# A hybrid attention block on one core: priority for the splits of the values, two heads written in place, a last block scaled on two engines, and residual scalings queued later

## The chip, the core and the metric

The kernel runs on one core of a Trainium2 chip. A core has a matrix engine (TensorE, PE in the profile, with its weight loads shown apart as PEld), a vector engine (VectorE, DVE), a scalar engine (ScalarE, ACT), a general engine (GpSimd, POOL) and a sync engine (SyncE, SP), which here issues nearly all DMAs. Matrix products are written to PSUM; everything else works from SBUF or PSUM; DRAM is reached by DMA. Each engine works through its own queue in order, and waits at its head for what it needs from the others. The metric is the device time of one execution in microseconds.

## The reference

One layer of a residual block, all in float32, on 512 positions of 2048 features:

```
h    = rmsnorm(x, g_attn)
proj = h @ w_in                       # 2048 x 6152: q, k, v of two kinds of heads, and f
o_sb  = stick_breaking_attention(qa, ka, va)       # 8 heads of 128, strictly causal
o_fox = forgetting_attention(qf, kf, vf, log_f)    # 8 heads of 128, causal
mixed = concat(head_rmsnorm(o_sb), head_rmsnorm(o_fox))
x = x + mixed @ w_out                 # 2048 x 2048
u = relu(rmsnorm(x, g_mlp) @ w_up)    # 2048 x 8192
x = x + (u * u) @ w_down              # 8192 x 2048
y = rmsnorm(x, g_final)
```

In stick-breaking attention the weight of a key is its logistic score times the product of (1 - score) of the keys between it and the query; in logarithms that is a running sum from right to left. Forgetting attention is a softmax with a bias that is the cumulative logarithm of a forget gate.

## The kernel before

**Precision.** Every operand of a product is split into a high part (a cast on ACT, line 60, or a scaled copy, line 63) and a low part (the difference, on DVE, line 61 or 64). `mm3` (lines 93 to 95) then makes three matmuls of high and low parts. One 512-column matmul is the unit of PE's work nearly everywhere.

**Order.** The program is written out without loops on the chip. A planner takes the instructions with their dependences and a priority each, which is program order, with blocks under `tc.high_priority()` ahead of everything else; it plays a modelled timeline and gives each engine, as it comes free, the ready instruction of the highest priority. The order so found is fixed for each engine's queue and for SP's. `with tc.issue_after(ins)` puts what the block holds on the engine of `ins` behind `ins` in that queue, without waiting for its end.

**Heads (lines 449 to 469).** The loop over `n` takes two heads a turn. `project` makes q and k of each (`project_q`, one PSUM bank `accq` of the pool `acc` of four banks, 48 matmuls). In turns 2, 6 and 10 `accumulate_v` makes the values of four heads at once in all four banks of `acc` (`accv`); in turn 14 it makes those of the last two. `take_v` splits them: for each of four row blocks and each pair of heads a scaled copy `vh` on ACT (line 63) and a low part `vl` on DVE (line 64). Only when both pairs of a row block are split is its bank free for the next `accq`. `attend` runs under high priority: `scores` into the one PSUM tile `s`, the weights `w` on ACT, DVE and POOL, transposes `pt` into the same PSUM tile, the split `ph`, `pl`, the product `o` with the values, and a norm (lines 291 to 303). Its result `os` is stored to DRAM, `md[h]` (line 304). Between the products, `drip` lets a side computation on DVE go on (`up_sums`, lines 153 to 161: sums of blocks of `w_up`, through two SBUF tiles `x0` and `x1`).

**Output projection (lines 512 to 555).** `mixed`, two tiles with the tags `x0` and `x1`, is loaded back from `md`, 16 DMAs (line 514). For each of four column blocks `n`, and each two heads `k0`, w_out is loaded and split, the two heads are split (`uh`, `ul`), and 24 matmuls add to `acco`. Column block 0 fills PE beside the last heads. Then x is added (line 534, DVE, `x2`), 16 transposes go to four PSUM tiles `tr`, ACT scales each by `g_up` into `hr` (line 547), and `a_form` makes the seven left-hand operands F of a Winograd form of the up projection, each with a split. Product 1 takes rows 0 to 255 of `hr` from the even transposes only; product 5 and its followers take sums of others. Squares of `x2` on ACT (line 555) follow. Of the last block, operands 4 and 3 are made later (line 761).

**Up and down projection (lines 579 to 827).** 32 `Unit`s make the hidden layer by seven products each (lines 619 and 621, 512 and 256 columns); PSUM tile `psa` is copied by ACT (line 625) between products 1, 6 and 7. The down projection takes the groups of `GROUPS` (two of three units, then six of four) for two halves `db`, each in seven products `second`, into two PSUM buffers `accd`; the first group copies them out on ACT (line 718), later ones add them on DVE (line 720).

**Residual.** The sum x2, stored in `xd`, is brought back in eight pieces by `add_residual` (lines 722 to 731): a load into a buffer `wraw` (three of them), two scalings by `v2` on ACT (line 728), one or two additions on DVE (729, 731). It is called from group 2 on, after the third product of each half, one piece at a time.

Of the kernel before, what the change touches and what calls it, by code (L numbers as in the profile page):

```python
# [11 lines left out]
ALU = mybir.AluOpType  # L12
# [23 lines left out]
def block_kernel(ctx, tc, x, g_attn, w_in, b_f, g_out_sb, g_out_fox, w_out, g_mlp, w_up, w_down, g_final, y):  # L36
# [16 lines left out]
    acc_cm = tc.tile_pool(name="acc", bufs=4, space=PSUM)  # L53
    acc = acc_cm.__enter__()

    lows = [None]

    def split(hi, lo, src, scale=None):
        if scale is None:
            ins = act.copy(hi, src)  # L60
            lows[0] = dve.tensor_tensor(lo, src, hi.bitcast(F32), op=ALU.subtract)  # L61
        else:
            ins = act.mul(hi, src, scale)
            dve.scalar_tensor_tensor(lo, src, scale, hi.bitcast(F32), op0=ALU.mult, op1=ALU.subtract)  # L64
        return ins
# [109 lines left out]
    with (  # L175
# [77 lines left out]
                pool.affine_select(out=d, in_=d, compare_op=op, fill=fill, base=0,  # L253
                                   pattern=[[0, n], [-1, P]] if n > 1 else [[-1, P]], channel_multiplier=1)

        def weigh(h, v, hc, w, gv, left=2):

            pt = atp.tile([P, 1536], F32, tag="s", name="pt")

# [43 lines left out]
            dve.scalar_tensor_tensor(os_, os_, gv, va, op0=ALU.mult, op1=ALU.mult)  # L303
            sp.dma_start(md[h], os_)

        def attend_sb(h, v, hc, q, k):
            s = scores(q, k)
            w = wide("w")
            act.activation(w, s, AF.Abs)
            act.activation(w, w, AF.Exp, scale=-1.0)  # L310
            act.activation(w, w, AF.Ln, bias=1.0)
            dve.scalar_tensor_tensor(w, s, 0.0, w, op0=ALU.max, op1=ALU.add)
            causal(w, ALU.is_gt, 0.0)
            for r in rows(w):

                dve.tensor_tensor_scan(r[:, ::-1], r[:, ::-1], r[:, ::-1], 0.0, op0=ALU.add, op1=ALU.max)
            dve.tensor_tensor(w, s, w, op=ALU.subtract)
            act.activation(w, w, AF.Exp)
            causal(w, ALU.is_gt, 0.0)
            weigh(h, v, hc, w, g_sb[:, h:h + 1], NH - 1 - h)  # L320

        def attend_fox(h, v, hc, q, k):
# [19 lines left out]
            weigh(NH + h, v, hc, w, g_fx[:, h:h + 1])  # L342

        o0 = 3 * WSB
        order = [NH + h for h in (6, 7, 0, 1, 2, 3, 4, 5)] + list(range(NH))
# [69 lines left out]
        with tc.tile_pool(name="attp", bufs=1, space=PSUM) as atp:  # L415
# [33 lines left out]
            for n in range(0, 2 * NH, 2):  # L449
# [5 lines left out]
                def attend(i, qk):  # L455
                    h = order[n + i]
                    with tc.high_priority():
                        (attend_fox if h >= NH else attend_sb)(h % NH, v, i, *qk)

                qk = [project(0), project(1)]  # L460

                if n == 2 * NH - 2:
                    vs = take_v(accumulate_v([v_columns(order[n])], 2 * P, [4] * 4))
                elif n % 4 == 2:
                    c = [v_columns(order[n + i]) for i in (0, 2)]
                    vs = take_v(accumulate_v(c[:1] if c[1] == c[0] + 2 * P else c, 4 * P, [2] * 8), 2)
                v = vs.pop(0)
                for i in range(2):
                    attend(i, qk[i])
# [39 lines left out]

    A_ORDER = (1, 4, 5, 6, 2, 7, 3)  # L510

    mixed = [mixp.tile([P, NH, NT], F32, tag=f"x{i}", name="mixed") for i in range(2)]
    for k in range(2 * NH):
        sp.dma_start(mixed[k // NH][:, k % NH, :], md[order[k]])

    for n in range(4):
        ns = slice(n * NT, (n + 1) * NT)
        ps = [acc.tile([P, NT], F32, tag="acc", name="acco") for _ in range(TB)]
# [14 lines left out]
        for t in range(TB):  # L533
            dve.tensor_tensor(x2[:, t, :], x2[:, t, :], ps[t], op=ALU.add)
        hr = xp.tile([P, 2, 2, NT], F32, tag="hr", name="hr")
        for i in range(4):
            tr = trp.tile([P, NT], F32, tag="tr", name="tr1")

            for t in ((TB - 1, *range(TB - 1)) if n < 3 else range(TB)):
# [4 lines left out]
                if i == 0 and t == TB - 1:  # L544
                    first_turn = turn_
            k = 4 * n + i
            act.mul(hr[:, i // 2, i % 2, :], tr, g_up[:, k:k + 1])
        sp.dma_start(xd[n], x2)
        s12 = xp.tile([P, 2, 2 * P], F32, tag="s12", name="s12")
        for p in (1, 5, 6, 2, 7, 4, 3):  # L550
            if n == 3 and p == 4:
                break
            a_form(p, hr, form_parts(p, n), s12)
        for t in range(TB):
            act.activation(x2[:, t, :], x2[:, t, :], AF.Square, accum_out=ss2[:, t, n:n + 1])
# [166 lines left out]
    def add_residual(p, db):  # L722
# [1 line left out]
        t0, j = {2: (0, 0), 3: (0, 1), 4: (1, 0), 7: (1, 1)}[p]  # L724
        r = wp.tile([P, 2, NT], F32, tag="wraw", name="xr")
        sp.dma_start(r, xd[2 * j + db][:, 2 * t0:2 * t0 + 2, :])
        for t in range(2):
            act.mul(r[:, t], r[:, t], v2[:, 2 * t0 + t:2 * t0 + t + 1])
        dve.tensor_tensor(M[p][:, :, db, :], M[p][:, :, db, :], r, op=ALU.add)
        if p == 7:  # L730
            dve.tensor_tensor(M[4][:, :, db, :], M[4][:, :, db, :], r, op=ALU.subtract)
# [198 lines left out]
```

## Time and profile before

| | us |
|---|---|
| median of three runs (2093.44, 2096.15, 2096.15) | 2096.15 |
| the profiled execution's own time | 2093.38 |
| its span | 2091.7 |

The span falls into stages, here with PE's idle time in each:

| stage | from, to (us) | PE idle | DVE busy | ACT busy |
|---|---|---|---|---|
| opening, first values | 0, 50 | 4.9 | 60% | 61% |
| heads | 50, 609 | 8.2 | 70% | 42% |
| output projection, last heads beside it | 609, 828 | 2.9 | 63% | 55% |
| up projection | 828, 1458 | 2.9 | 81% | 65% |
| down projection | 1458, 2037 | 5.9 | 86% | 43% |
| end | 2037, 2091.7 | 9.1 | 62% | 36% |

The mean granted clock of PE over the span is 0.996. To read the tables: a stage in which PE is idle for 1% of the time is set by PE's own work, and what can be changed there is only where and why it stands still. In rows of the timeline the columns are the start, the duration, engine and line, operation, what it writes and reads, and in brackets the idle time of the engine just before with what ended it. In tables by stretch the columns are the stretch, its length, busy time and number of instructions of PE, PEld, DVE, ACT and POOL, the granted clock, the DMA share and GB/s.

### The profile page before, as it was taken

How to read it: one execution, taken by the hardware profiler on the slowest of the kernel's cores; microseconds unless marked ns; L12 is line 12 of the kernel's file. 1: busy time of each engine (PE TensorE's matmuls, PEld its weight loads, DVE VectorE, ACT ScalarE, POOL GpSimd, SP SyncE). 2: the span in 40 equal slices, each digit the busy share in tenths (PEclk: the TensorE clock that was granted, in tenths of full speed). 3: DMA queues.
4: the chain of work that ended last, by engine and by line, in shares of the span. 5: the costliest groups of instructions: out<-in, count | busy, mean ns of one | idle time of the engine just before them, and what ended most of it. 6: DMA issues, size and time to landing. Idle time of an engine off the chain costs nothing.

```text
span 2091.7 us, 26837 instructions
## 1 busy us (share of the span) xinstructions
PE 2057.8 (98%) x10292; PEld 1748.8 (84%) x10292; DVE 1604.4 (77%) x1825; ACT 1068.5 (51%) x1428; POOL 65.5 (3%) x77
## 2 busy tenths in 40 slices
PE   9999999998999999999999999999999999999998
PEld 8888888887888787888888888888788888888886
DVE  6767767676866565788788787788698988888886
ACT  6334343354455555666666666666644443333433
POOL 0000000010110000000000000000000000000003
PEclk9999999999999999999999999999999999999999
DMA  8997986966843444577777787788856665664731
GB/s 252 338 321 220 327 269 215 338 190 228 292 153 100 161 135 154 195 260 258 247 265 258 242 267 249 249 266 301 281 202 248 247 223 176 245 246 140 266 116 81
DMA packets 361761, 482.10 MB, mean 230 GB/s; under 512 B 12017, under 2 KB 255777, under 8 KB 351521
## 3 DMA queue, kind: packets, MB, share of 16 engines
q1 hardware_dynamic: 360672, 478.26, 68.1%
q10 hardware_dynamic: 960, 2.13, 0.3%
q8 instruction: 81, 1.33, 0.3%
q14 instruction: 48, 0.39, 0.1%
HBM read 360.28 MB, written 120.06 MB: 230 GB/s over the span
## 4 chain that ended last, share of the span: by engine, by line
PE 90%; DVE 4%; DMA 3%; ACT 1%; issue 1%; SPq 0%; ACTq 0%; DVEq 0%
PE psa L619 11%; PE accd L94 7%; PE accd L95 7%; PE accd L93 7%; PE psa L621 6%; PE accq L93 5%; PE psc L619 5%; PE accq L95 5%; PE accq L94 5%; PE psc L621 3%; PE acco L93 3%; PE acco L95 3%; PE acco L94 3%; PE psb L619 3%; PE accv L93 3%; PE accv L95 2%
## 5 line engine op out<-in xcount | busy, mean ns | idle before, releaser
L61 DVE TENSOR_TENSOR wl<-wu,wh 128x1024 fp32r<-128x1024 f32 x166 | 201.7, 1219 | 35.0 <-ACT wh L60 21.3
L60 ACT CAST wh<-wd 128x1024 fp32r<-128x1024 f32 (+1 forms) x136 | 134.5, 999 | 165.3 <-PE accd L95 105.4
L60 ACT CAST wh<-wraw 128x1024 fp32r<-128x1024 f32 (+2 forms) x133 | 135.5, 1019 | 157.9 <-PE accq L94 86.5
L60 ACT CAST wh<-wu 128x1024 fp32r<-128x1024 f32 x166 | 173.7, 1049 | 79.4 <-PE psa L619 19.0
L93 PE MATMUL accq<-hH,wh 128*128 128x512 f32 x512 | 201.1, 393 | 7.7 <-DVE vl L64 7.7
L95 PE MATMUL accq<-hH,wl 128*128 128x512 f32 x512 | 201.2, 393 | 0.0
L94 PE MATMUL accq<-hL,wh 128*128 128x512 f32 x512 | 200.6, 392 | 0.0
L61 DVE TENSOR_TENSOR wl<-wraw,wh 128x1024 fp32r<-128x1024 f32 (+2 forms) x133 | 157.7, 1187 | 49.0 <-ACT wh L60 48.6
L61 DVE TENSOR_TENSOR wl<-wd,wh 128x1024 fp32r<-128x1024 f32 (+1 forms) x136 | 155.6, 1153 | 44.5 <-ACT wh L60 43.9
L93 PE MATMUL accd<-wh,uf 128*128 128x512 f32 x436 | 169.8, 390 | 1.0 <-issue 1.0
L94 PE MATMUL accd<-wl,uf 128*128 128x512 f32 x436 | 169.6, 389 | 0.0
L95 PE MATMUL accd<-wh,uf 128*128 128x512 f32 x436 | 169.6, 389 | 0.0
L60 ACT CAST wx<-wd 128x1024 fp32r<-128x1024 f32 (+1 forms) x88 | 87.6, 1000 | 125.2 <-PE accd L95 73.0
L93 PEld LDWEIGHTS accq<-hH,wh 128*128 128x128 f32 x512 | 96.7, 189 | 28.2 <-issue 8.5
L61 DVE TENSOR_TENSOR wx<-wd,wx 128x1024 fp32r<-128x1024 f32 (+1 forms) x88 | 100.7, 1153 | 21.3 <-ACT wx L60 21.0
L93 PE MATMUL accd<-wx,uf 128*128 128x512 f32 x284 | 110.6, 390 | 3.4 <-ACT m L718 3.4
L94 PEld LDWEIGHTS accq<-hL,wh 128*128 128x128 f32 x512 | 96.7, 189 | 19.9
L95 PEld LDWEIGHTS accq<-hH,wl 128*128 128x128 f32 x512 | 96.6, 189 | 19.9
L94 PE MATMUL accd<-wx,uf 128*128 128x512 f32 x284 | 110.6, 390 | 0.2 <-DVE wx L61 0.2
L720 DVE TENSOR_TENSOR m<-m,accd 128x1024 f32<-128x1024 f32 x84 | 102.1, 1216 | 11.0 <-PE accd L95 10.9
L95 PE MATMUL accd<-wx,uf 128*128 128x512 f32 x284 | 110.5, 389 | 0.0
L619 PE MATMUL psa<-fl,wh 128*128 128x512 f32 x388 | 107.0, 391 | 2.6 <-DVE fl L61 2.6
(312 smaller groups left out, 4865.5 us busy)
## 6 DMA issues: line engine op xcount, KB each, us to landing
ufd<-st SPq DMA_DIRECT2D x98, 512.0 KB, 5.2
sums<-in_w_up_dram SPq DMA_DIRECT2D x96, 512.0 KB, 6.0
td<-sums SPq DMA_DIRECT2D x32, 1536.0 KB, 8.2
wd<-in_w_down_dram SPq DMA_DIRECT2D x48, 1024.0 KB, 7.1
wu<-td SPq DMA_DIRECT2D x95, 512.0 KB, 4.9
wraw<-in_w_in_dram SPq DMA_DIRECT2D x84, 512.0 KB, 5.9
uf<-ufd SPq DMA_DIRECT2D x42, 1024.0 KB, 6.9
wu<-in_w_up_dram SPq DMA_DIRECT2D x32, 1024.0 KB, 7.8
```

The source lines that it names most:

```text
L60: ins = act.copy(hi, src)
L61: lows[0] = dve.tensor_tensor(lo, src, hi.bitcast(F32), op=ALU.subtract)
L93: pe.matmul(out, sh, mh, start=first, stop=False, skip_group_check=True)
L94: pe.matmul(out, sh, ml, start=False, stop=False, skip_group_check=True)
L95: pe.matmul(out, sl, mh, start=False, stop=last, skip_group_check=True)
L619: pe.matmul(ps, hi[:, a, :], both, start=a == 0 and p in (1, 2, 5), stop=False, skip_group_check=True)
L621: pe.matmul(ps[:, :2 * P], lo[:, a, :], F[p][a // 4][:, a % 4, 0, :], start=False, stop=a == KC // 2 - 1, skip_group_check=True)
L720: dve.tensor_tensor(M[p][:, :, db, :], M[p][:, :, db, :], ps, op=ALU.add)
```

## The change

There are four edits.

1. The splits of `take_v` in turns 2, 6, 10 and 14 are traced under `tc.high_priority()`, as the attention is. The products of the values before them are not.
2. `mixed` is allocated in turn 14, before the last two heads' attention, and 14 of the 16 loads stand there. The last two heads write the last step of their norm (line 303) straight into `mixed[1]`, without store and load.
3. In the last of the four column blocks the transposes are taken in the order 0, 2, 1, 3; tiles 1 and 3 are scaled on DVE (`tensor_scalar`) instead of ACT; and `a_form(1)` is traced right after tile 2, ahead of tiles 1 and 3. The remaining operands follow in the same order as before.
4. The two scalings of `add_residual` are put behind the last unscaled cast that `split` made (`casts[0]`), which at that point of the program is a cast of the same half's third product. The loads and additions are not bound.

```diff
-    lows = [None]
+    lows, casts = [None], [None]
@@ def split
-            ins = act.copy(hi, src)
+            ins = casts[0] = act.copy(hi, src)
@@ def weigh
-            dve.scalar_tensor_tensor(os_, os_, gv, va, op0=ALU.mult, op1=ALU.mult)
-            sp.dma_start(md[h], os_)
+            out = os_ if here is None else here
+            dve.scalar_tensor_tensor(out, os_, gv, va, op0=ALU.mult, op1=ALU.mult)
+            if here is None:
+                sp.dma_start(md[h], os_)
@@ def attend
-                        (attend_fox if h >= NH else attend_sb)(h % NH, v, i, *qk)
+                        (attend_fox if h >= NH else attend_sb)(h % NH, v, i, *qk, mixed[1][:, NH - 2 + i, :] if n == 2 * NH - 2 else None)
...
                 if n == 2 * NH - 2:
-                    vs = take_v(accumulate_v([v_columns(order[n])], 2 * P, [4] * 4))
+                    ps = accumulate_v([v_columns(order[n])], 2 * P, [4] * 4)
+                    with tc.high_priority():
+                        vs = take_v(ps)
+                    mixed = [mixp.tile([P, NH, NT], F32, tag=f"x{i}", name="mixed") for i in range(2)]
+                    for k in range(2 * NH - 2):
+                        sp.dma_start(mixed[k // NH][:, k % NH, :], md[order[k]])
                 elif n % 4 == 2:
                     c = [v_columns(order[n + i]) for i in (0, 2)]
-                    vs = take_v(accumulate_v(c[:1] if c[1] == c[0] + 2 * P else c, 4 * P, [2] * 8), 2)
+                    ps = accumulate_v(c[:1] if c[1] == c[0] + 2 * P else c, 4 * P, [2] * 8)
+                    with tc.high_priority():
+                        vs = take_v(ps, 2)
...
-    mixed = [mixp.tile([P, NH, NT], F32, tag=f"x{i}", name="mixed") for i in range(2)]
-    for k in range(2 * NH):
-        sp.dma_start(mixed[k // NH][:, k % NH, :], md[order[k]])
@@ for n in range(4)
-        for i in range(4):
+        last = n == 3
+        for i in (0, 2, 1, 3) if last else range(4):
             tr = trp.tile([P, NT], F32, tag="tr", name="tr1")
...
             k = 4 * n + i
-            act.mul(hr[:, i // 2, i % 2, :], tr, g_up[:, k:k + 1])
+            if last and i % 2:
+                dve.tensor_scalar(hr[:, i // 2, i % 2, :], tr, g_up[:, k:k + 1], None, op0=ALU.mult)
+            else:
+                act.mul(hr[:, i // 2, i % 2, :], tr, g_up[:, k:k + 1])
+            if last and i == 2:
+                a_form(1, hr, form_parts(1, n))
         sp.dma_start(xd[n], x2)
         s12 = xp.tile([P, 2, 2 * P], F32, tag="s12", name="s12")
-        for p in (1, 5, 6, 2, 7, 4, 3):
-            if n == 3 and p == 4:
-                break
+        for p in (5, 6, 2, 7) if last else (1, 5, 6, 2, 7, 4, 3):
             a_form(p, hr, form_parts(p, n), s12)
@@ def add_residual
-        for t in range(2):
-            act.mul(r[:, t], r[:, t], v2[:, 2 * t0 + t:2 * t0 + t + 1])
+        with tc.issue_after(casts[0].ins):
+            for t in range(2):
+                act.mul(r[:, t], r[:, t], v2[:, 2 * t0 + t:2 * t0 + t + 1])
```

More of the change, by code (lines that the diff above doesn't have):

```diff
@@ L254, in causal, with weigh @@
                                    pattern=[[0, n], [-1, P]] if n > 1 else [[-1, P]], channel_multiplier=1)
-        def weigh(h, v, hc, w, gv, left=2):
+        def weigh(h, v, hc, w, gv, here, left=2):
             pt = atp.tile([P, 1536], F32, tag="s", name="pt")
@@ L302, in weigh, with attend_sb @@
             dve.scalar_tensor_tensor(va, va, 1.5, ra, op0=ALU.subtract, op1=ALU.mult)
-            dve.scalar_tensor_tensor(os_, os_, gv, va, op0=ALU.mult, op1=ALU.mult)
-            sp.dma_start(md[h], os_)
-        def attend_sb(h, v, hc, q, k):
+            out = os_ if here is None else here
+            dve.scalar_tensor_tensor(out, os_, gv, va, op0=ALU.mult, op1=ALU.mult)
+            if here is None:
+                sp.dma_start(md[h], os_)
+        def attend_sb(h, v, hc, q, k, here):
             s = scores(q, k)
@@ L319, in attend_sb, with attend_fox @@
             causal(w, ALU.is_gt, 0.0)
-            weigh(h, v, hc, w, g_sb[:, h:h + 1], NH - 1 - h)
-        def attend_fox(h, v, hc, q, k):
+            weigh(h, v, hc, w, g_sb[:, h:h + 1], here, NH - 1 - h)
+        def attend_fox(h, v, hc, q, k, here):
             ck = atp.tile([P, NT], F32, tag="o", name="ck")
@@ L341, in attend_fox @@
                 dve.tensor_scalar(r, r, l[:, i:i + 1], None, op0=ALU.mult)
-            weigh(NH + h, v, hc, w, g_fx[:, h:h + 1])
+            weigh(NH + h, v, hc, w, g_fx[:, h:h + 1], here)
         o0 = 3 * WSB
```

## The prediction, made before the changed kernel was run

> **What bounds the kernel now.** I read three views in this order: the engines' busy time, PE's waits by line, and short stretches behind each wait. The page's first part:
>
> ```profile
> PE 2057.8 (98%) x10292; PEld 1748.8 (84%) x10292; DVE 1604.4 (77%) x1825; ACT 1068.5 (51%) x1428; POOL 65.5 (3%) x77
> ```
>
> PE is the bound nearly everywhere: of 2091.7 us it stands still for 33.9. No edit takes work off PE, so all there is to win lies in those 33.9 us and in what follows them. PE's waits, longest first:
>
> ```profile
> PE accq L93 <- DVE vl L64: 7.7, 1, 7.7
> PE accd L93 <- ACT m L718: 3.4, 2, 2.1
> PE trg L353 <- DMA g_rows<-in_g_attn_dram: 3.3, 1, 3.3
> PE acco L93 <- ACT uh L60: 2.9, 1, 2.9
> PE psa L619 <- DVE fl L61: 2.6, 1, 2.6
> ```
>
> Four of these five are what the edits touch, one each: I call them S1 (7.7, low parts of values), S2 (2.9, heads read back), S3 (2.6, the last block's first operand) and S4 (2.1, a copy on ACT); the fifth is the opening. A wait costs more than itself. In stretches of 2 us (the figure before the DMA share is the granted clock) right behind S1, S2, S3 and S4, with a calm stretch last:
>
> ```profile
> 500.00:502.00 2.00, 2.00 (x5) 1.62 (x6) 2.00 (x4) 0.66 (x1) 1.11 (x2) 0.50 0.64 190
> 502.00:504.00 2.00, 2.00 (x6) 1.52 (x6) 1.94 (x4) 0.00 (x0) 0.00 (x0) 0.52 1.07 442
> 688.00:690.00 2.00, 2.00 (x7) 1.53 (x6) 0.15 (x1) 0.58 (x1) 0.00 (x0) 0.56 0.79 305
> 690.00:692.00 2.00, 2.00 (x7) 1.52 (x6) 2.00 (x4) 0.91 (x2) 0.00 (x0) 0.59 0.00 0
> 834.00:836.00 2.00, 1.51 (x7) 1.39 (x8) 2.00 (x4) 2.00 (x7) 0.00 (x0) 0.75 1.07 354
> 836.00:838.00 2.00, 2.00 (x9) 1.81 (x9) 2.00 (x5) 2.00 (x7) 0.00 (x0) 0.50 1.11 375
> 838.00:840.00 2.00, 2.00 (x13) 1.82 (x12) 1.74 (x5) 2.00 (x3) 0.00 (x0) 0.89 1.02 413
> 1484.00:1486.00 2.00, 1.15 (x5) 0.97 (x6) 0.22 (x1) 2.00 (x3) 0.00 (x0) 1.00 1.05 409
> 1700.00:1750.00 50.00, 50.00 (x222) 41.39 (x221) 46.96 (x36) 21.92 (x23) 0.00 (x0) 1.00 0.77 281
> ```
>
> PE counts as busy in them, but at half clock. The lost time is the missing clock times the length: S1 2 x (0.50 + 0.48) = 2.0; S2 2 x (0.44 + 0.41) = 1.7; S3 2 x (0.25 + 0.50 + 0.11) = 1.7; S4 nothing. So the four cost 9.7, 4.6, 4.3 and 2.1, together 20.7 us.
>
> The Trainium skill (TensorE: Matmul & The Clock Gate, section "Why this matters for your kernels") says that idle gaps over about 3 us bring the clock down to half. By that rule the gaps of S2 and S3 would have cost only themselves and the four together 17.3 us. The trace differs: the clock was 0.56 behind a wait of 2.9 us and 0.50 behind one of 2.6, and I go by the trace.
>
> **Edit 1, the splits of the values.** S1 in detail, DVE's queue first:
>
> ```profile
> 488.20 0.47 ACT L63 ACTIVATE vh<-accv,r1v 128x256 fp32r<-128x256 f32 x1
> ```
> ```profile
> 488.96 1.54 DVE L158 TENSOR_TENSOR sums<-sums 128x1024 f32<-128x1024 f32 x1
> 490.42 0.77 DVE L61 TENSOR_TENSOR pl<-ph,pl 128x512 fp32r<-128x512 f32 x1
> 491.12 2.64 DVE L316 TENSOR_TENSOR_SCAN w<-w 128x256 f32<-128x256 f32 x3
> 493.69 0.45 DVE L64 SCALAR_TENSOR_TENSOR vl<-accv,r1v,vh 128x256 fp32r<-128x256 f32 x1
> ```
> ```profile
> 499.22 0.86 DVE L64 SCALAR_TENSOR_TENSOR vl<-accv,r1v,vh 128x256 fp32r<-128x256 f32 x2
> ```
> ```profile
> 491.75 0.40 PE L297 MATMUL ssq<-pl,onesr 128*128 128x512 f32 x1
> 499.83 0.77 PE L93 MATMUL accq<-hH,wh 128*128 128x512 f32 x1 [7.68 <-DVE vl L64]
> ```
>
> The first high part of the values is there at 488.67; its low part waits 5 us behind a block sum, an attention split and scans, and the bank's last low part runs at 499.22, while PE wants the bank at about 492.1. With priority the first low part goes ahead of the block sum, at about 489.0; the second cast and low part (0.47 and 0.45 us) follow by about 490.9 even behind the `pl` of 0.77. The bank is free 1.2 us before PE asks. S1 goes: -9.7; if the planner leaves the order, 0. Nothing is added; block sums move back, and nobody waits for them here. The eight casts wait on ACT for PE's rows of values, as they do now; behind them stand casts of projection weights, one of which serves 24 matmuls, 24 x 50/222 = 5.4 us. The scans yield to at most eight low parts, 8 x 0.45 = 3.6 us: the head gets that much later in its place, and is priced as a rival.
>
> **Edit 2, two heads in place.**
>
> ```profile
> 678.60 0.74 DVE L303 SCALAR_TENSOR_TENSOR os_last<-os_last,g_rest,ph 128x512 f32<-128x512 f32 x1
> ```
> ```profile
> 679.37 0.34 SPq L304 DMA_DIRECT2D md<-os_last  x1
> 683.32 0.34 SPq L514 DMA_DIRECT2D mixed<-md  x1
> ```
> ```profile
> 686.13 0.62 ACT L60 CAST uh<-mixed 128x512 fp32r<-128x512 f32 x1 [1.80 <-DMA mixed<-md]
> ```
>
> The last head is finished at 679.34; store and load take until 686.13. In place, its cast can end at 679.34 + 0.7 = 680.0, while PE has other work until 686.80 - 2.90 = 683.9. The wait goes with 3.9 us to spare: -4.6; at worst 0, if the head itself comes late against PE (a rival). Four DMAs leave SP. The 14 other loads stand earlier in program order, past the last two heads' stores on SP's queue, but need the tiles that `sums` holds until its last use, so they cannot start sooner than now; each costs SP 0.34 us.
>
> **Edit 3, the last block.**
>
> ```profile
> 828.82 2.42 ACT L547 ACTIVATE hr<-tr,g_rest 128x512 f32<-128x512 f32 x4 [5.81 <-PE tr L543]
> ```
> ```profile
> 831.28 0.69 DVE L501 TENSOR_TENSOR s<-hr 128x512 f32<-128x512 f32 x1 [3.19 <-ACT hr L547]
> ```
> ```profile
> 834.49 0.80 PE L619 MATMUL psa<-fl,wh 128*128 128x512 f32 x2 [2.61 <-DVE fl L61]
> ```
> ```profile
> 837.12 0.58 ACT L625 COPY s<-psa 128x512 f32<-128x512 f32 x1
> ```
> ```profile
> 838.95 1.09 PE L619 MATMUL psa<-fh,wh 128*128 128x512 f32 x4
> ```
> ```profile
> 2086.47 0.48 DVE L870 TENSOR_SCALAR m<-m,v 128x512 f32<-128x512 f32 x1
> ```
>
> Four scalings of 0.61 run in a row, then sums, then splits, until PE gets the low part at 834.49; it wanted it at 831.9. Now ACT scales two tiles by 828.82 + 1.21 = 830.0, casts operand 1 (0.62) by 830.7, DVE subtracts (0.69) by 831.4: in time. DVE's two scalings from PSUM occur nowhere in the trace; the nearest rows are 0.48 (the same operation from SBUF) and 0.69 (an addition of that size). I take 0.69, the longer, as these read PSUM; both end at about 830.2 beside ACT's, so DVE's sums start 1.1 us sooner than at 831.28. What is late next: before product 6 PE needs ACT's copy of `psa`, now at 837.12 to 837.70 behind an unbroken row of ACT's work. PE comes 4.3 us sooner, at 838.95 - 4.3 = 834.7; the copy comes only by the two scalings sooner, at 837.7 - 1.2 = 836.5. A wait of 1.8 us stays, of S4's size, which left the clock alone. So -2.5, with 0 and -4.3 as ends.
>
> **Edit 4, the residual.**
>
> ```profile
> 1477.09 1.57 ACT L60 CAST wx<-wd 128x1024 fp32r<-128x1024 f32 x2
> 1482.57 1.33 ACT L728 ACTIVATE xr<-xr,v 128x512 f32<-128x512 f32 x2 [3.92 <-DMA xr<-xd]
> 1483.81 0.99 ACT L718 COPY m<-accd 128x1024 f32<-128x1024 f32 x1
> ```
> ```profile
> L729 DVE TENSOR_TENSOR m<-m,xr 128x1024 f32<-128x1024 f32 x8 | 9.8, 1220 | 0.0
> ```
>
> ACT takes up a scaling in group 0, waits 3.92 us for its load, and the copy that frees `accd` stands behind it. Queued behind a cast of group 2, some 100 us later, the scaling finds its data landed, and the copy runs at 1478.7: -2.1. The first three loads hold all three `wraw` buffers that much longer; what else uses them stands earlier in the program or in the last group. The additions (1.22 us, ten with line 731's) spread over eight halves instead of bunching; with DVE at 46.96 of 50 us in the calm stretch, a pair may hold PE up: between -2.1 and +2.4, and I take -2.1, since the row of L729 shows no idle time and PE did not stop at any of its eight. The other 1.3 us on line 718 stay.
>
> **Sum.** 9.7 + 4.6 + 2.5 + 2.1 = 18.9 off the profiled execution's 2093.38 gives 2074.5. The median of the runs shown is 2096.15, 2.8 above it, and I do not know on which side the next median falls: half of that, 2076. All four in full would be 2093.4 - 20.7 = 2072.7.
>
> **Rivals.**
>
> *A. The chain of the last heads becomes the bound.* The heads follow one another through the single PSUM tile of scores. If the last one still ends at 679.34 although PE saves S1, PE resumes at 680.05 instead of 686.80: S1 and S2 together bring only 6.8. With 2.5 and 2.1: 2093.4 - 11.4 = 2082.0. Against it:
>
> ```profile
> 500.73 1.11 POOL L253 TENSOR_SCALAR_AFFINE_SELECT w<-w 128x384 f32<-128x384 f32 x2 [10.07 <-ACT w L318]
> ```
> ```profile
> 506.42 1.25 PE L263 MATMUL pt<-ident,w 128*128 128x128 f32 x10
> ```
>
> The weights were done at 501.84 and PE transposed them at 506.42: the head waited 4.6 us for its turn on PE, so it gains when PE is earlier. For it: PE runs dry at 683.9 - 9.7 = 674.2, so the heads that follow must make up 680.0 - 674.2 = 5.8 us between them.
>
> *B. The change does not do what it says at S1.* Priority ranks only what is ready; if the modelled times put scans and sums first as now, S1 stays: 4.6 + 2.5 + 2.1 = 9.2, or 2084.2. Against it: the block sum that went first has no priority.
>
> *C. Slower: the splits lengthen the head's chain.* At the values of turn 10 eight casts (0.47) and eight low parts (0.45) go ahead of a head's steps, 7.4 us, and ACT may stand a step of the product (5.4 us) waiting for PE's rows; at turn 14 half of it, 6.4. Together up to 19.2 us: the last head ends at 698.5, PE resumes at 699.2, 12.4 later than now; less 2.5 and 2.1 that is +7.8, or 2101. It decides from a delay of 11.4 us on; between 7 and 15 it gives no change. Against it: the casts can run while the head is on DVE or POOL, and the low parts while it is on ACT or POOL.
>
> **Chances.** Forecast 0.60, A 0.16, B 0.10, C 0.14, of which 0.08 ends within 0.2% and 0.06 slower. A measurement of this kernel tells about 0.2%, 4 us, from no change. Faster 0.60 + 0.16 + 0.10 = 0.86, same 0.08, slower 0.06. The range runs from 2070 (all four in full, and the 1.3 us with some clock) to 2087 (B with the median's 2.8); it leaves out C and a little on either side.
>
> **What would show it.** S1: no wait of `accq` on `vl`, `vl` right behind each `vh`, and no half clock near 500. S2: `uh` of the last head cast within 1 us of line 303; the wait on `mixed` gone. If PE stands there on line 303 or a later step of the last head, A is right. S3: operand 1's low part by 831.5 on the old scale, and a short wait on line 625's copy before product 6; a wait of over 2.5 us there, or on another `fl`, makes it wrong. S4: no scaling before group 2, no 2.1 us on line 718, and no new wait on line 720. A new wait over 3 us elsewhere makes the sum wrong by that and about 1.7 us of clock.

## The result and the profile after

The changed kernel takes 2087.18 us in the median of five runs (2084.63 to 2091.71), the kernel before, beside it on the same chip, 2095.57 (2093.44 to 2096.15): a ratio of 0.9964, 95% interval 0.9949 to 0.9978. That is 8.4 us less where the prediction's sum had 18.9, and 0.2 us above its range. The profiled execution is the longest of the five, 2091.71 us with a span of 2090.0.

PE's waits in the changed kernel, longest first (us in total, times, longest):

```profile
PE accq L93 <- DVE vl L64: 7.7, 1, 7.7
PE pt L263 <- DVE w L343: 3.8, 1, 3.8
PE trg L355 <- DMA g_rows<-in_g_attn_dram: 3.3, 1, 3.3
PE tr L190 <- DMA x<-in_x_dram: 2.3, 1, 2.3
PE psa L628 <- DVE fl L61: 1.8, 1, 1.8
PE accd L93 <- ACT m L727: 1.2, 1, 1.2
```

Of the four waits that the edits were to remove, S2 is gone, S3 is 1.8 instead of 2.6, of S4's two only the one of 1.2 is left, and S1 stands untouched at 7.7. The wait on `w`, 0.5 before, is 3.8. DVE's queue around the values of turn 10, and PE's matmul behind it, in the changed kernel:

```profile
495.57 1.54 DVE L158 TENSOR_TENSOR sums<-sums 128x1024 f32<-128x1024 f32 x1
497.04 0.77 DVE L61 TENSOR_TENSOR pl<-ph,pl 128x512 fp32r<-128x512 f32 x1
497.74 2.64 DVE L318 TENSOR_TENSOR_SCAN w<-w 128x256 f32<-128x256 f32 x3
500.30 0.45 DVE L64 SCALAR_TENSOR_TENSOR vl<-accv,r1v,vh 128x256 fp32r<-128x256 f32 x1
```
```profile
505.83 0.86 DVE L64 SCALAR_TENSOR_TENSOR vl<-accv,r1v,vh 128x256 fp32r<-128x256 f32 x2
```
```profile
506.45 0.76 PE L93 MATMUL accq<-hH,wh 128*128 128x512 f32 x1 [7.69 <-DVE vl L64]
```

It is the queue of before, item by item, 6.6 us later: block sum, `pl`, three scans, first low part. Up to the last two heads, every engine of the two programs issues the same instructions in the same order. What differs before that point is not the change's doing.

To see where time went, I took the starts of four instructions that every variant has, and the differences between them: the low part of the tenth head's weights, the first addition of the last residual block, the last Square of the hidden units, and the last multiplication. Before (the fourth row, 2086.47, stands in the prediction), then after:

```profile
474.09 1.49 DVE L61 TENSOR_TENSOR pl<-pt,ph 128x1280 fp32r<-128x1280 f32 x1 [1.41 <-ACT ph L60]
```
```profile
824.18 1.28 DVE L534 TENSOR_TENSOR x<-x,acco 128x512 f32<-128x512 f32 x2
```
```profile
1471.15 1.06 ACT L647 ACTIVATE c<-c 128x1024 f32<-128x1024 f32 x1
```
```profile
480.70 1.49 DVE L61 TENSOR_TENSOR pl<-pt,ph 128x1280 fp32r<-128x1280 f32 x1 [1.41 <-ACT ph L60]
```
```profile
827.16 1.28 DVE L539 TENSOR_TENSOR x<-x,acco 128x512 f32<-128x512 f32 x2
```
```profile
1472.56 1.06 ACT L656 ACTIVATE c<-c 128x1024 f32<-128x1024 f32 x1
```
```profile
2084.84 0.48 DVE L880 TENSOR_SCALAR m<-m,v 128x512 f32<-128x512 f32 x1
```

So the stretch that holds S1 and S2 went from 350.09 to 346.46 us (-3.6, predicted -14.3), the one with S3 from 646.97 to 645.40 (-1.6, predicted -2.5), the one with S4 from 615.32 to 612.28 (-3.0, predicted -2.1). Together -8.2, close to the 8.4 between the medians. The stretch ahead of them took 6.6 us longer in this one execution. The reason is in DVE's waits for block sums, before and then after:

```profile
232.00 1.23 DVE L158 TENSOR_TENSOR sums<-sums 128x1024 f32<-128x1024 f32 x1 [3.48 <-DMA sums<-in_w_up_dram]
244.44 1.23 DVE L158 TENSOR_TENSOR sums<-sums 128x1024 f32<-128x1024 f32 x1 [1.46 <-DMA sums<-in_w_up_dram]
```
```profile
235.81 1.23 DVE L158 TENSOR_TENSOR sums<-sums 128x1024 f32<-128x1024 f32 x1 [4.92 <-DMA sums<-in_w_up_dram]
249.15 1.23 DVE L158 TENSOR_TENSOR sums<-sums 128x1024 f32<-128x1024 f32 x1 [5.38 <-DMA sums<-in_w_up_dram]
```

The same loads landed later, DVE stood 5.4 us longer for these two (4.92 and 5.38 against 3.48 and 1.46), and the head's weights behind them in its queue came 3.8 us late to PE (0.5 before), with half clock after it. The other profiles bear this out. Twelve of the fourteen kernels issue the same instructions up to here; in their profiles the two waits of DVE sum to between 4.9 and 10.3 us, and PE's wait on `w` rises with the sum by and large, from 0.5 at 4.9 over 1.3 at 7.1 and 2.4 at 7.9 to 3.8 at 9.6 and 10.3. The last experiment takes DVE's waits away altogether.

All runs in one table. The four columns of stretches are differences to the profile of before, from the same four instructions; the ratio is that of the timed runs, with its interval. One profile carries the accidents of one execution, the first stretch above all; the ratio does not.

| kernel | to the 10th head | S1, S2 | S3, up | S4, down | median us (before) | ratio |
|---|---|---|---|---|---|---|
| changed | +6.6 | -3.6 | -1.6 | -3.0 | 2087.2 (2095.6) | 0.9964 [0.9949, 0.9978] |
| priority_alone | +0.3 | -0.1 | +0.8 | +1.4 | 2096.3 (2096.2) | 0.9996 [0.9987, 1.0005] |
| heads_alone | +1.6 | -3.6 | +2.2 | -4.1 | 2087.0 (2096.2) | 0.9960 [0.9947, 0.9974] |
| block_alone | +1.1 | -1.2 | -2.3 | -2.8 | 2089.5 (2097.2) | 0.9963 [0.9950, 0.9975] |
| residual_alone | +1.2 | +0.2 | -0.2 | -2.9 | 2091.5 (2097.2) | 0.9977 [0.9966, 0.9987] |
| changed_without_residual | +1.8 | -4.2 | -2.1 | -1.9 | 2088.7 (2097.2) | 0.9961 [0.9948, 0.9973] |
| casts_paired | +1.3 | -5.7 | -3.3 | -3.0 | 2085.3 (2096.2) | 0.9945 [0.9933, 0.9958] |
| values_staged | +3.7 | -6.0 | -1.4 | -3.0 | 2085.2 (2096.2) | 0.9947 [0.9933, 0.9960] |
| staged_tail | +6.1 | -9.2 | -1.2 | -2.9 | 2085.5 (2097.2) | 0.9940 [0.9926, 0.9953] |
| operand_first | +3.3 | -4.1 | -0.7 | -2.9 | 2089.0, one run (2097.8) | |
| operand_and_copy_first | +0.7 | -4.7 | -1.9 | -3.0 | 2084.4, one run (2097.8) | |
| all_found | +3.3 | -10.7 | -1.6 | -3.0 | 2081.2 (2097.8) | 0.9920 [0.9906, 0.9935] |
| block_sums_left_out | -11.5 | -3.7 | -2.1 | -4.1 | 2072.3 (2097.8) | 0.9878 [0.9861, 0.9894] |

In block_sums_left_out the tenth head stands earlier among PE's products (2250 matmuls begun before it, 2299 in the kernel before), so its first two columns count only together, -15.2.

### The profile page after: what moved, and what is told of

Same layout as the page of the kernel before. It is cut to its first block, busy times and chain, and to the rows that moved or that the text cites. A ratio compares the mean times of both kernels' runs of the same rounds, so it can differ in the third digit from the quotient of the medians.

```text
span 2090.0 us, 26829 instructions
## 1 busy us (share of the span) xinstructions
PE 2058.1 (98%) x10292; PEld 1749.7 (84%) x10292; DVE 1606.5 (77%) x1827; ACT 1067.4 (51%) x1426; POOL 65.2 (3%) x77
## 4 chain that ended last, share of the span: by engine, by line
PE 94%; DMA 2%; DVE 2%; ACT 1%; issue 1%; SPq 0%; ACTq 0%; DVEq 0%
PE psa L628 11%; PE accd L93 8%; PE accd L94 8%; PE accd L95 8%; PE psa L630 5%; PE accq L93 5%; PE accq L95 5%; PE accq L94 5%; PE psc L628 5%; PE acco L93 3%; PE acco L94 3%; PE acco L95 3%; PE psc L630 3%; PE psb L628 3%; PE accv L93 3%; PE accv L95 3%
```

## The experiments

### Edit 1 alone, then the wait itself

**priority_alone** is the kernel before with this:

```diff
-                    vs = take_v(accumulate_v(c[:1] if c[1] == c[0] + 2 * P else c, 4 * P, [2] * 8), 2)
+                    ps = accumulate_v(c[:1] if c[1] == c[0] + 2 * P else c, 4 * P, [2] * 8)
+                    with tc.high_priority():
+                        vs = take_v(ps, 2)
```

> The kernel before with edit 1 alone (the splits of the values of turns 2, 6, 10 and 14 get attention's priority). Theory 'readiness': the planner hands each engine the instruction that is ready first in its modelled times, and priority only ranks those that are ready together; the low parts are not, so every engine keeps its order, accq waits 7.7 us on vl and the time is that of before (within 4 us). Rival 'priority works but is masked by the other edits': vl runs right behind vh, the wait of 7.7 goes, and the time falls by about 9.7 us, to 2086.

The ratio is 0.9996 and PE's wait on `vl` 7.7. No instruction of any engine changed its place. So edit 1 by itself does nothing, neither alone nor beside the others. That the low parts are not yet ready in the planner's modelled times when it hands out the scans is my explanation of it. No run shows the modelled times.

**casts_paired** leaves the priority and changes which instruction waits for which:

```diff
-                for i, (vh, vl) in enumerate(vs):
-                    split(vh[:, t, :], vl[:, t, :], ps[t][:, i * 2 * P:(i + 1) * 2 * P], r1[:, t:t + 1])
+                parts = [(vh[:, t, :], vl[:, t, :], ps[t][:, i * 2 * P:(i + 1) * 2 * P]) for i, (vh, vl) in enumerate(vs)]
+                for hi, _, src in parts:
+                    act.mul(hi, src, r1[:, t:t + 1])
+                for hi, lo, src in parts:
+                    dve.scalar_tensor_tensor(lo, src, r1[:, t:t + 1], hi.bitcast(F32), op0=ALU.mult, op1=ALU.subtract)
```

> The changed kernel, but of each bank of values both casts come ahead of both low parts. Theory 'turns in the bank': in the changed kernel the second cast starts at 500.79 only when the first low part has read the bank (500.30 + 0.45), and its own low part then finds 2.7 us of other work (1.21 and 1.48) ahead of it; with the casts together both low parts follow the scans at about 500.7 + 0.9 = 501.6 where the bank was free at 506.4, so the wait falls from 7.7 to about 2.8 us and the time by 4.9, or 6 with some of the half clock. Rival 'DVE's queue alone': the second low part stands as far back as before, the wait stays near 7.7 and the time is the same.

DVE's queue and PE's matmul in casts_paired, then the longest of PE's waits there:

```profile
492.36 2.96 DVE L321 TENSOR_TENSOR_SCAN w<-w 128x256 f32<-128x256 f32 x4
495.24 1.62 DVE L221 SCALAR_TENSOR_TENSOR vl<-accv,r1v,vh 128x256 fp32r<-128x256 f32 x4
```
```profile
496.23 0.47 PE L93 MATMUL accq<-hH,wh 128*128 128x512 f32 x1 [3.04 <-DVE vl L221]
```
```profile
PE acco L93 <- ACT uh L60: 3.5, 1, 3.5
```

Four low parts now run in a row behind the scans, and the wait is 3.0, as the theory of the turns in the bank has it. In the changed kernel the second cast waited for the first low part, as ACT's row there shows:

```profile
500.79 0.47 ACT L63 ACTIVATE vh<-accv,r1v 128x256 fp32r<-128x256 f32 x1 [0.46 <-DVE vl L64]
```

Both read one bank, in turns. The second cast was done at 501.26, and its low part, the first of the two at 505.83, then found all of this ahead of it on DVE, 4.6 us together (the expectation counted 2.7 of it):

```profile
501.38 1.21 DVE L159 TENSOR_TENSOR sums<-sums 128x1024 f32<-128x1024 f32 x1
502.51 0.86 DVE L64 SCALAR_TENSOR_TENSOR vl<-accv,r1v,vh 128x256 fp32r<-128x256 f32 x2
503.30 1.21 DVE L61 TENSOR_TENSOR wl<-wraw,wh 128x1024 fp32r<-128x1024 f32 x1
504.43 1.48 DVE L319 TENSOR_TENSOR w<-s,w 128x1280 f32<-128x1280 f32 x1
```

But in casts_paired the wait of `acco` on `uh`, which edit 2 had removed, is back with 3.5 us, and the stretch is only 2.1 us shorter than in the changed kernel, not 4.9.

**values_staged** takes DVE out of the bank's release altogether (turn 10 only):

```diff
+                if staged:
+                    src = at.tile([P, NT], F32, tag="vf", name="vf", bufs=2)
+                    act.mul(src, ps[t], r1[:, t:t + 1])
                 for i, (vh, vl) in enumerate(vs):
-                    split(vh[:, t, :], vl[:, t, :], ps[t][:, i * 2 * P:(i + 1) * 2 * P], r1[:, t:t + 1])
+                    split(vh[:, t, :], vl[:, t, :], src[:, i * 2 * P:(i + 1) * 2 * P], None if staged else r1[:, t:t + 1])
...
-                        vs = take_v(ps, 2)
+                        vs = take_v(ps, 2, n == 10)
```

> The changed kernel, but at turn 10 ACT first copies each finished bank of values, scaled, to SBUF, and the casts and low parts read the copy: the bank no longer waits for DVE. Theory 'DVE's queue': the first bank is free one ACT operation (about 0.65 us) behind PE's last row, near 495.5, before PE asks for it at 498.8; no wait of accq, no half clock, 9.7 us less than the changed kernel. Rival 'the last heads become the bound' (rival A of the prediction): the wait at 498.8 goes, but PE stands again before it reads the last heads near 680, and of the 9.7 only about 2 are left. Second rival 'ACT pays': the four copies delay the casts of the next weights and the head, and a new wait of 1 to 3 us appears within 20 us behind.

PE does not wait for the values any more, and again 3.5 us appear in front of the last heads. The stretch with S1 and S2 is 6.0 us shorter than before, against 14.3 if both had gone: that is rival A of the prediction, which gave 6.8 for the two. The heads did not gain from PE's earlier start. Here are the low part of the tenth head's weights and the last product of the last head in values_staged, to set beside those at 474.09 and 678.60 before:

```profile
477.79 1.49 DVE L61 TENSOR_TENSOR pl<-pt,ph 128x1280 fp32r<-128x1280 f32 x1 [1.40 <-ACT ph L60]
681.84 0.75 DVE L308 SCALAR_TENSOR_TENSOR mixed<-os_last,g_rest,ph 128x512 f32<-128x512 f32 x1
```

From the one to the other it takes 204.1 us, and 204.5 before. PE spent the time it had saved on the output projection instead, whose first matmul comes 149.8 us after the tenth head and 164.0 before. The head right behind the values even comes 3.8 us later than before (38.7 us after the tenth, 34.9 before) and the later heads make that up. That the single PSUM tile of scores is what holds the heads to their pace, as rival A has it, no run tests. What else keeps the last head late shows in its own chain, on DVE, PE and ACT of values_staged:

```profile
671.89 0.69 DVE L61 TENSOR_TENSOR pl<-ph,pl 128x512 fp32r<-128x512 f32 x1
```
```profile
676.20 0.39 PE L300 MATMUL oq<-pl,onesr 128*128 128x512 f32 x1
```
```profile
677.12 0.39 PE L301 MATMUL oq<-pl,onesr 128*128 128x512 f32 x1
```
```profile
677.87 0.68 ACT L302 ACTIVATE ra_last<-oq,eps 128x512 f32<-128x512 f32 x1
```
```profile
683.29 0.79 PE L93 MATMUL acco<-wh,uh 128*128 128x512 f32 x1 [3.52 <-ACT uh L60]
```

The sum of squares has its operand at 672.6, but its second matmul stands in PE's queue until 677.1 behind products of the output projection. Before, it waited as long (operand at 668.5, second matmul at 673.1), but there was time for it. PE fills its own later gap too early.

**staged_tail** adds this to values_staged:

```diff
+                with ExitStack() as behind:
+                    if n == 0 and (k0 == 12 or k0 == 10 and t == 3):
+                        behind.enter_context(tc.issue_after(tail[0].ins))
                     for i in range(2):
...
```

> The kernel of values_staged, but the last 30 products of the output projection's first tile that need no last head are queued on PE behind the last head's sum of squares. Theory 'the last head's chain is the bound once the values do not hold PE up': in values_staged the operand of that sum was ready at 672.6, PE took it at 676.2 to 677.5 behind products queued ahead, and the chain of eight steps behind it (Ln, Exp, Square, three on DVE, a cast, 5.0 us in a row) ended 3.5 us too late; taken at once it ends at about 680.4 where PE asks at about 680.2, so the wait of acco on uh falls from 3.5 to under 1 us, its half clock goes, and the time falls by 3 to 5 us against values_staged. Rival 'the chain is late from its start': the head's scores or weights come late, PE stands at the sum of squares instead, and nothing is gained.

(`tail[0]` is the second matmul of the sum of squares, the last one traced.) The wait on `uh` is gone, and the stretch 3.2 us shorter than in values_staged. PE now stands 1.7 us at the sum of squares itself:

```profile
673.85 0.50 PE L300 MATMUL oq<-pl,onesr 128*128 128x512 f32 x1 [1.71 <-ACT pl L60]
```

Thirty products behind it were too many; all_found holds back 24. The 3 to 5 us do not show in the medians (2085.5 and 2085.2); the two intervals, each over 5 us wide, still hold a difference of 3.

### Edits 2, 3 and 4 by themselves

**heads_alone** is the kernel before with edit 2 only:

```diff
+            out = os_ if here is None else here
+            dve.scalar_tensor_tensor(out, os_, gv, va, op0=ALU.mult, op1=ALU.mult)
+            if here is None:
+                sp.dma_start(md[h], os_)
...
```

> The kernel before with edit 2 alone (the last two heads written in place). By the comparison of the two traces this edit brought 4.45 us: the wait of 2.9 of acco on uh goes with its half clock, and the time is 4.5 us less than before, about 2091. Rival 'it only showed because another wait came earlier in that execution': PE still stands for over 1 us on a step of the last heads.

The wait on `uh` goes as expected; the ratio, 0.9960, is as good as that of the whole change. The table shows one reason: S4's stretch is 4.1 us shorter without edit 4. ACT's queue there, in heads_alone:

```profile
1478.02 1.03 ACT L721 COPY m<-accd 128x1024 f32<-128x1024 f32 x1
```
```profile
1479.87 1.35 ACT L731 ACTIVATE xr<-xr,v 128x512 f32<-128x512 f32 x2
```

The planner, given another program ahead of it, put the copy of `accd` in front of the scaling of `xr`. Before, the same copy stood behind that scaling and its wait of 3.92 for the load. S3's stretch is 2.2 us longer in this profile; 1.4 of that is the half clock behind the wait on `fl`, which cost 3.1 us here and 1.7 before (last section).

**block_alone** and **residual_alone** are the kernel before with edit 3 or edit 4 only:

```diff
+            if last and i % 2:
+                dve.tensor_scalar(hr[:, i // 2, i % 2, :], tr, g_up[:, k:k + 1], None, op0=ALU.mult)
+            else:
+                act.mul(hr[:, i // 2, i % 2, :], tr, g_up[:, k:k + 1])
...
```
```diff
+        with tc.issue_after(casts[0].ins):
+            for t in range(2):
+                act.mul(r[:, t], r[:, t], v2[:, 2 * t0 + t:2 * t0 + t + 1])
```

> The kernel before with edit 3 alone (last residual block scaled on two engines, operand 1 split ahead). By the two traces it brought 2.25 us: the wait of psa on fl falls from 2.6 to about 1.8 us and the half clock behind it goes. Theory: the same here, 2 to 3 us less in the stretch from 826 to 900 than before. Rival 'the clock, not the order': the wait is as in the changed kernel but the half clock appears all the same, and only about 1 us is left.

> The kernel before with edit 4 alone (residual scalings queued behind a cast of a later group). The wait of 2.1 of accd on m goes, 3 us less by the two traces between 1460 and 1500. Rival 'the additions bunch': a new wait of PE on DVE near 1600 to 1640 takes 1 us or more of it back.

Edit 3 brings 2.3 us in its stretch, edit 4 brings 2.9 in its own, and PE gets no new wait from the additions. In block_alone S4's stretch is 2.8 us shorter as well, and there too edit 4 is absent. Its stretch with S1 and S2 is 1.2 us shorter though neither edit is there: behind its wait of 2.7 on `uh` the clock stayed full.

**changed_without_residual** is the changed kernel with edit 4 undone.

```diff
-        with tc.issue_after(casts[0].ins):
-            for t in range(2):
-                act.mul(r[:, t], r[:, t], v2[:, 2 * t0 + t:2 * t0 + t + 1])
+        for t in range(2):
+            act.mul(r[:, t], r[:, t], v2[:, 2 * t0 + t:2 * t0 + t + 1])
```

> The changed kernel without edit 4. In heads_alone the wait of 2.1 on the copy was gone without edit 4: the planner's new order there put the copy ahead of the scaling. Theory 'the planner's order, not edit 4, decides': here the scaling stands behind the copy too (two copies earlier than the wait of before), the wait of 2.1 stays away, and the time is that of the changed kernel within 1 us. Rival 'edit 4 brings its 2 to 3 us': the wait of about 2.1 is back and the time is 2 to 3 us longer than the changed kernel's.

The ratio is 0.9961 to 0.9964 with edit 4: no difference. S4's longer wait stays away in all three kernels that have edit 2 or 3 and not edit 4. The stretch is 1.1 us longer than with edit 4 in these two profiles, which the times do not tell from nothing. So the ratios of the edits don't add up, in part at least because three of them cure the same wait.

### What holds the last block, and the loads of the sums

**operand_first** pins the split of operand 1 ahead of the weights of product 6 and of the sums; **operand_and_copy_first** also queues the four squares behind the copy of `psa`.

```diff
+            with ExitStack() as behind:
+                if last:
+                    behind.enter_context(tc.issue_after(first[1]))
+                a_form(p, hr, form_parts(p, n), s12)
...
+                if self.u == 0 and p == 6:
+                    for ins in first:
+                        behind.enter_context(tc.issue_after(ins))
                 split(hi, lo, self.b[p])
...
+                with tc.issue_after(copies[0].ins):
+                    for t in range(TB):
+                        act.activation(x2[:, t, :], x2[:, t, :], AF.Square, accum_out=ss2[:, t, 3:4])
```

> The changed kernel, but on ACT and DVE the split of operand 1 of the last block stands ahead of the weights of product 6 and of the sums. Theory of the prediction ('the copy is next'): operand 1 is complete at about 834.2 where PE asks for it at 834.9 on the changed kernel's scale, the wait of 1.8 on fl goes, and PE comes 1.8 us earlier to product 6, whose copy of psa still stands behind four squares on ACT (end at 839.5): the wait there grows from 0.3 to about 2.1 us and nothing is gained. Rival 'the copy has slack': the wait on the copy stays under 1 us and the stretch from 826 to 900 is 1 to 2 us shorter.

> operand_first, and the four squares of the last block are queued on ACT behind the copy of psa. Theory 'the copy is next': both waits go, 1.5 to 2 us less than the changed kernel between 826 and 900. Rival 'a third wait follows', on operand 5 or 6 (fl behind sums and weights on DVE): 1 us or more of PE's wait is left.

PE's wait in operand_first, then in operand_and_copy_first:

```profile
834.85 0.74 PE L636 MATMUL psc<-fl,wh 128*128 128x512 f32 x2 [2.37 <-DVE fl L61]
```
```profile
831.05 1.19 PE L636 MATMUL psa<-fh,wh 128*128 128x512 f32 x4 [1.71 <-ACT s L642]
```

The wait of 1.8 on operand 1 only moves: to operand 5, which DVE splits behind sums and weights, and then to the copy, which stands on ACT behind a cast of `hr` that waits for DVE. The theory of the copy fails in the first of them: nothing is gained, as it said, but the wait there is not on the copy. In the second over 1 us of wait is left, as the rival of a third wait had it, but on the copy and not on operand 5 or 6. The stretch was -0.7 and -1.9 where the changed kernel has -1.6. One run each shows no gain.

**all_found** joins values_staged, the sum of squares ahead of 24 products, and operand_and_copy_first. The line of staged_tail that differs:

```diff
-                    if n == 0 and (k0 == 12 or k0 == 10 and t == 3):
+                    if n == 0 and k0 == 12:
```

> values_staged, the last head's sum of squares ahead of 24 products of the first tile (not 30), and operand_and_copy_first. If the three theories hold together: no wait of accq on vl, of acco on uh and of psa on fl or s over 0.5 us; between 454 and 712 about 9 to 10 us less than the kernel before, between 826 and 900 about 4, between 1460 and 1640 about 3; 2080 in the median, 7 us less than the changed kernel. Rival 'something else becomes late each time', as with the last heads: at most 3 us less than the changed kernel.

The median is 2081.18 where 2080 was expected, the ratio 0.9920; its interval, 0.9906 to 0.9935, lies below that of the changed kernel, 0.9949 to 0.9978. PE waits neither on `vl` nor on `uh` any more, and 0.7 and 0.3 us at the sum of squares; the stretch with S1 and S2 is 10.7 us shorter than before. The last block still has a wait of 1.7 us on the copy of `psa`, and its stretch is 1.6 us shorter than before where about 4 were expected, so the gain comes from the values and the heads.

**block_sums_left_out** is the changed kernel without DVE's subtractions for the up projection, which then has wrong operands; its time is there to be read, not to be reached.

```diff
-            yield dve.tensor_tensor(b11, b12, b11, op=ALU.subtract)
-            yield dve.tensor_tensor(b12, b22, b12, op=ALU.subtract)
-            dve.tensor_tensor(b22, b22, b11, op=ALU.subtract)
+            yield
+            yield
```

> The changed kernel without DVE's three subtractions of each unit's block sums in the attention (their loads and stores stay; the up projection computes with wrong sums). Theory 'the loads of the sums make the difference between executions': DVE then waits for no load there, the stall of pt on w near 274 (0.2 to 3.8 us in the profiles so far, in programs alike up to it) is under 0.6, and the executions lie within 3 us of each other. Theory on the values' wait: 2.7 us of sums (1.54 and 1.21) leave DVE between the casts and the last low part, so the wait of 7.7 falls to 5 or less. Rival 'other DMAs or PE's clock': stall and spread stay as they were.

The four runs lie between 2071.73 and 2072.53, 0.8 us apart, where the changed kernel's five span 7.1. Longest of PE's waits here:

```profile
PE trg L354 <- DMA g_rows<-in_g_attn_dram: 3.3, 1, 3.3
PE tr L189 <- DMA x<-in_x_dram: 2.1, 1, 2.1
PE psa L627 <- DVE fl L61: 1.8, 1, 1.8
```

Neither `w` nor `vl` is among them. With the twelve profiles above this shows that DVE's waits for the sums' loads make the stretch up to the tenth head differ from one execution to the next. That they make all of the spread is argued: this kernel also takes 96 operations off DVE, and from 38 us on every queue but POOL's has another order. For the same reason it can't say what the sums cost the values: the wait there went whole, 7.7 us and not the 2.7 of the two sums that stand in it.

## Why the prediction was wrong, step by step

- **Edit 1, the step that failed.** The prediction put it: "With priority the first low part goes ahead of the block sum, at about 489.0". It did not; the order stayed, and 9.7 of the 18.9 us with it. The argument set against rival B, "the block sum that went first has no priority", looked at whose priority was higher and not at whether the planner ever compared the two. That the order stayed is shown, by every queue of priority_alone; why the planner left it is open. Rival B's sum, 9.2 off, is near the 8.4 measured, in part by luck: its terms 4.6, 2.5 and 2.1 came out at 3.6, 1.6 and 3.0. It had a chance of 0.10.
- **Edit 1, behind that.** Had the order changed, the sum would most likely still have been wrong. With the values' wait cut to 3.0 or removed by other means, S1 and S2 together brought 5.7 and 6.0 us, not 14.3, since the last heads' chain then ends too late: rival A, which said 6.8. The argument set against it, that a head waiting for its turn on PE gains when PE is earlier, failed: the last head's last product came 204.1 us after the tenth head's weights, 204.5 before. What rival A did not see is that 4.5 us of this are a wait of the last sum of squares in PE's queue, behind work that PE could have kept for the gap; holding that work back brought 3.2 of them.
- **Edit 2.** Right: no wait for a load of `mixed`, no wait of `acco` on `uh`. In the changed kernel the last head's product of line 304 runs at 686.03 and its cast at 686.81, within 1 us of it. The stretch gives -3.6 instead of -4.6, because the half clock behind the 7.7 us, which stayed, was 0.9 us longer in that execution.
- **Edit 3.** The size was near (-1.6 in its stretch, -2.25 between the same matmuls near 830 and 930, for -2.5), the reason half right. A wait of 1.8 us stayed, but on operand 1's low part, which the step had "by 831.4: in time", and not on the copy. The half clock went, in part by luck: behind the same wait it cost 1.7 us in values_staged and block_sums_left_out. DVE's queue in the changed kernel shows the step that was missed, two sums and the weights put ahead of it, so that it was done at 836.5, or 833.5 on the scale of before (3.0 us less):

```profile
832.02 1.41 DVE L554 TENSOR_SCALAR hr<-tr,g_rest 128x512 f32<-128x512 f32 x2 [0.95 <-PE tr L549]
833.53 0.69 DVE L510 TENSOR_TENSOR s<-hr 128x512 f32<-128x512 f32 x1
834.14 1.22 DVE L61 TENSOR_TENSOR wl<-wu,wh 128x1024 fp32r<-128x1024 f32 x1
835.28 0.68 DVE L514 TENSOR_TENSOR hr<-hr 128x512 f32<-128x512 f32 x1
835.88 1.89 DVE L61 TENSOR_TENSOR fl<-hr,fl 128x512 fp32r<-128x512 f32 x3
```

  The scalings on DVE took 1.41 for two, 0.7 each, as assumed.
- **Edit 4.** The stretch is 3.0 shorter for 2.1 predicted, and the wait of 1.2 stayed as said. What was wrong is the credit: without edit 4 the planner's new order removes the same wait.
- **The 1.4 us for the median.** The median of before came out 2.2, 2.8, 3.8 and 4.4 us above its profiled execution in four groups of runs, not half of 2.8: that execution was one of the quicker ones.

## What to carry to other kernels

A planner's priority is worth nothing until the order of the issued instructions is seen to change: look at the queue, and if it is the same, cut the dependency (stage the bank, put both casts first) or pin the order. A chain that ends just in time becomes the bound when the wait ahead of it goes, so price two waits on one path together and look for what stands in front of the late chain's steps on the engine that will wait for it. And test each edit alone: any edit shifts a planner's order elsewhere, and a wait may vanish for that reason.

## What the runs showed of the hardware

How long a wait lasts does not settle whether the clock halves behind it. The fourteen profiles hold 58 waits of PE of over 1 us between 60 and 2000 us, taken with the granted clock in the 16 us behind each. The 22 of 1.02 to 1.72 us cost nothing. Of the nine of 1.76 to 1.92, three cost 1.71 us of missing clock and six nothing. Of the fourteen of 2.06 to 3.10, ten cost 1.71, one 3.1 and three nothing. The four of 3.52 to 3.80 cost 1.71 to 3.04, the nine of 7.7 1.86 to 3.08. The commonest price, 1.71, is 3.41 us at half clock.

What settles it is how the wait falls on a grid of time. The traces hold the moments at which the granted clock changes. In each of the fourteen profiles they lie on one grid of 3.413 us, to within 0.004 us, and the grid starts at another point in each execution. The 27 stretches of half clock between 60 and 2000 us are one, two or three steps of it long. I took PE's idle time in each of these steps, its length less PE's busy time. Of the 7899 steps that ran at full clock, all 25 with 1.92 us of idle time or more were followed by a step at half clock, and none of the 7871 with 1.75 or less. Three lie between: those of 1.76 and 1.77 were followed by half clock, that of 1.80 was not. Of the 45 steps at half clock, the 18 with 0.61 us of idle time or more were followed by another one, the 27 without any by full clock.

Here are the steps around the wait of 3.04 in casts_paired, which the grid cut into 1.24 and 1.80, and around the wait of 1.76 in block_sums_left_out, which fell into one step. The second figure is PE's busy time, the one before the DMA share the granted clock:

```profile
491.01:494.42 3.41, 2.18 (x10) 1.46 (x8) 3.41 (x5) 2.51 (x6) 0.88 (x1) 1.00 1.13 341
494.42:497.83 3.41, 1.60 (x7) 1.37 (x8) 3.41 (x7) 1.96 (x4) 0.00 (x0) 1.00 0.44 132
497.83:501.25 3.42, 3.42 (x17) 2.81 (x16) 3.42 (x7) 0.19 (x1) 0.00 (x0) 1.00 0.00 0
```
```profile
815.99:819.40 3.41, 1.65 (x10) 1.08 (x9) 3.41 (x6) 3.41 (x8) 0.00 (x0) 1.00 0.92 273
819.40:822.82 3.42, 3.42 (x17) 3.23 (x16) 3.32 (x9) 3.36 (x9) 0.00 (x0) 0.50 1.12 384
822.82:826.23 3.41, 3.41 (x21) 3.00 (x21) 3.41 (x4) 2.00 (x4) 0.00 (x0) 1.00 1.02 405
```

The longer wait kept the full clock, and the shorter one lost it. So about half a step of idle time brings the clock down. A wait between some 1.8 and 3.8 us costs it or not by where it falls on the grid, which differs from one execution to the next; the same wait of 2.61 on `fl` cost 1.7 us in three profiles and 3.1 in heads_alone.

The Trainium skill (TensorE: Matmul & The Clock Gate, section "What's actually happening") says that the clock follows PE's activity in windows of 3413 ns that run freely. The grid of 3.413 us in these traces agrees.
